# Attention scores of a hybrid decoder trunk: the keys' low parts meet the queries' high parts alone, for two heads at a time

## The chip, the cores and the metric

The kernel runs on one core of a Trainium2 chip. The metric is the time that one execution takes on the device, in microseconds. A core has five engines that work side by side, each with a queue of its own: TensorE (PE in the profile; its loads of the stationary operand are listed as PEld), VectorE (DVE), ScalarE (ACT), GpSimd (POOL) and SyncE (SP), which starts transfers. Matmuls write to PSUM, which the kernel uses as eight buffers of 128 partitions by 512 float32.

## What is computed

A trunk of two layers on a sequence of 512 tokens with 1024 features, in float32. Layer 0 mixes a gated linear recurrence and retention, layer 1 is sparse attention with three branches, and each layer ends with a SwiGLU block. The change is in the attention of layer 1 alone. Cut to that, for a block of queries (16 heads of 64 features in 4 groups of 4, keys and values shared by a group):

```python
s = einsum('bqgrd,bngd->bgrqn', qb, kc)            # compressed blocks
p_cmp = where(vis, softmax(where(vis, s, NEG)), 0)
...
s = einsum('bqgrd,bqgkld->bgrqkl', qb, kg)         # selected blocks
p_slc = softmax(where(ok, s, NEG))
...
s = einsum('bqgrd,bkgd->bgrqk', qb, kw)            # sliding window
p_win = softmax(where(band, s, NEG))
o = gate0 * o_cmp + gate1 * o_slc + gate2 * o_win
```

There are 512 / 64 = 8 blocks to select from, and up to 16 are selected, so all are; the window is 512 as well. The second and third branch are therefore plain causal attention, each with keys and values of its own.

## The kernel before

Matmuls run in a fast float32 form that keeps fewer bits, so an operand is split into a high part and a low part (the rest), and a product is made of three: high by high, high by low, low by high (`mm3`, L196 to L203). Weights are read from DRAM by SyncE's and GpSimd's queues and split by ScalarE and VectorE (`split`, L129).

**Keys and queries.** `layer1` (L937) makes the keys of the two causal branches. Each key head is written twice, in partitions 0 to 63 and again in 64 to 127 (`twice`, used at L1085), and the transposed tiles KH (high) and KL (low) are filled at L1099 to L1101. `stack` (L1113) writes the queries QS so that the two halves of the partitions hold different parts: an even head has its high part in partitions 0 to 63 and its low part in 64 to 127, an odd head the other way round (L1119 to L1122). One matmul over 128 partitions of QS against KH is thus high by high plus low by high; one against KL is high by low plus low by low.

**Units, heads, blocks.** `attention` (L1186) works through tiles i of 128 queries in the order 2, 3, 1, 0. A unit is a tile i, a group g and a set of branches: for i of 2 or 3 one branch (16 units in all), for i of 1 or 0 both branches side by side (8 units). A unit has four heads. With i + 1 blocks of 128 keys for each branch, a head's scores are 384 wide at i = 2, 512 at i = 3, 2 x 256 at i = 1 and 2 x 128 at i = 0. The steps of a head are:

- `head_s` (L1259): three matmuls into a PSUM buffer of the four behind `psA`: queries by KH (L1268), queries by KL (L1269), and the causal mask, added by an identity matmul on the last block of each branch (L1270);
- `head_m` (L1272): VectorE takes the negated row maximum (L1274);
- `head_e` (L1276): ScalarE's exponential with row sums, one for each branch (L1278);
- `scale` (L1285): GpSimd multiplies with the gate over the sum (L1288), a unit later.

The steps of a block of 128 keys, three units later (LAG at L1343), are `block_t` (L1290: four transposes into one of two PSUM buffers, L1293), `block_hi` (ScalarE's copy, L1297), `block_lo` (VectorE's subtraction, L1300, the last reader of that PSUM buffer) and `block_v` (L1303: two matmuls with the values, L1308 and L1309).

**Order.** The loop at L1346 to L1397 writes these steps slot by slot, a head (sl = 0 to 3) and a block in each slot:

```python
head_s(*hd)                      # slot sl of unit n
block_t(*bl)                     # a block of unit n - LAG
with prio(offset=12): head_m(*hd)
block_hi(*bl)
with prio(offset=-6): head_e(*hd)
with prio(offset=-12): block_lo(*bl)
```

Behind these, still in the slot, stand the scaling of the unit before, a `block_v`, steps of the compressed branch and of the finished outputs (`advance`), and, early in the stage, a piece of the queries' projection (`fill`, L201 to L203). This is not yet each engine's queue. When the program is built, a scheduler goes through its own forecast of the run and gives each engine the ready instruction that comes first in this order, shifted by the offsets of `prio`. A matmul that stands earlier but becomes ready late can thus be put between two that stand together here.

Two other places of the kernel matter for the change. `retention_core` (L613) multiplies 64-row halves at L633, for lower and upper partitions in turn, between full products at L650. The compression of keys has two small 64-row matmuls at L1055.

Of the kernel before, what the change touches and what calls it, by code (L numbers as in the profile page):

```python
# [19 lines left out]
AF = mybir.ActivationFunctionType  # L20
ALU = mybir.AluOpType
AX = mybir.AxisListType
PSUM = bass.MemoryType.PSUM

P = 128
# [10 lines left out]
DH = 64  # L36
# [27 lines left out]
class Trunk:  # L64
# [1121 lines left out]
    def attention(self, QS, stack, stacked, qlate, halves, KH, KL, VV, kc2, vc, gate, OH, OL, fill):  # L1186
# [3 lines left out]
        V, A, Q, T = nc.vector, nc.scalar, nc.gpsimd, nc.tensor  # L1190
# [52 lines left out]
        def late(t):  # L1243
            QS[t] = self.b8([P, H, P], F32R, name="qs")
            for c in range(2):
                stack(t, qlate[:, halves[1].index(t), 8 * c:8 * c + 8, :].rearrange("p h d -> p (h d)"), c)
                yield
# [11 lines left out]
        def head_s(u, r):  # L1259
            if r == 0:  # L1260
                u.p = self.probs().rearrange("p (r b x) -> p r b x", r=R, b=u.n)
                u.rs = self.sm.tile([P, R, u.n], F32, tag="rs", name="rs")
                u.kh, u.kl = (x[u.g // 2][:, u.bs[0]:u.bs[-1] + 1, u.g % 2, 0:u.nk] for x in (KH, KL))
            h = R * u.g + r
            ps = self.psA("ps_s")
            u.ps = ps[:, 0:u.n * u.nk].rearrange("p (b x) -> p b x", b=u.n)
            q = QS[u.i][:, h, :]
            T.matmul(u.ps, q, u.kh, start=True, stop=False)  # L1268
            T.matmul(u.ps, q, u.kl, start=False, stop=False)  # L1269
            T.matmul(u.ps[:, :, u.i * P:u.nk], self.identr, self.triNeg.unsqueeze(1).broadcast_to([P, u.n, P]), start=False, stop=True)  # L1270

        def head_m(u, r):  # L1272
            u.nm = self.sm.tile([P, 2], F32, tag="nm", name="nm")
            V.tensor_reduce(u.nm[:, 0:u.n], u.ps, axis=AX.X, op=ALU.max, negate=True)  # L1274

        def head_e(u, r):  # L1276
            for b in range(u.n):
                A.activation(u.p[:, r, b, 0:u.nk], u.ps[:, b, :], AF.Exp, bias=u.nm[:, b:b + 1], accum_out=u.rs[:, r, b:b + 1])  # L1278

        def norm(u):  # L1280
            gb = gate[:, u.i, :].rearrange("p (h b) -> p h b", b=3)[:, R * u.g:R * u.g + R, u.bs[0] + 1:u.bs[-1] + 2]
            V.reciprocal(u.rs, u.rs)
            Q.tensor_tensor(u.rs, u.rs, gb, op=ALU.mult)

        def scale(u, r):  # L1285
            for b in range(u.n):
                x = u.p[:, r, b, 0:u.nk]
                Q.tensor_tensor(x, x, u.rs[:, r, b:b + 1].broadcast_to([P, u.nk]), op=ALU.mult)  # L1288

        def block_t(u, b, j):  # L1290
            u.pt = self.psC("ps_tr")
            for r in range(R):
                T.transpose(u.pt[:, r * P:(r + 1) * P], u.p[:, r, b, j * P:(j + 1) * P], self.ident)  # L1293
            u.th, u.tl = (self.g2([P, S], F32R, name="pt" + n) for n in "hl")

        def block_hi(u, b, j):
            A.copy(u.th, u.pt)  # L1297

        def block_lo(u, b, j):
            V.tensor_tensor(u.tl, u.pt, u.th.bitcast(F32), op=ALU.subtract)  # L1300
            u.last = u.th, u.tl

        def block_v(u, b, j, th, tl):  # L1303
            br = u.bs[b]
            k = (u.i, u.g)
            if br == 0 and j == 0:
                out_ps[k] = self.psB("ps_o")
            T.matmul(out_ps[k], VV[br][:, j, u.g, :], th, start=(br == 0 and j == 0), stop=False)  # L1308
            T.matmul(out_ps[k], VV[br][:, j, u.g, :], tl, start=False, stop=False)  # L1309
            if br == 1 and j == u.i:  # L1310
                while u.i not in cmp_pt:
                    advance()
                ch, cl = cmp_pt[u.i]
                T.matmul(out_ps[k], vc[:, u.g, :], ch, start=False, stop=False)
                T.matmul(out_ps[k], vc[:, u.g, :], cl, start=False, stop=True)

        def finish(i, g):
            po = out_ps.pop((i, g))
            up = self.g2([P, S], name="up")
            A.copy(up[0:DH], po[DH:P])  # L1320
            yield
            o = self.g2([P, 2, P], name="o")
            p5, u5 = (x.rearrange("p (k z c) -> p k z c", k=2, z=2) for x in (po, up))
            for par in range(2):
                V.tensor_tensor(o[par * DH:(par + 1) * DH], p5[0:DH, :, par, :], u5[0:DH, :, par, :], op=ALU.add)
            yield
            c = slice(2 * (g % 2), 2 * (g % 2) + 2)
            oh, ol = (x[g // 2][:, c, i * P:(i + 1) * P] for x in (OH, OL))
            A.copy(oh, o)
            yield  # L1330
            Q.tensor_tensor(ol, o, oh.bitcast(F32), op=ALU.subtract)
            yield
# [5 lines left out]
        def advance():  # L1338
            if side and next(side[0], 0) == 0:
                side.pop(0)  # L1340
                advance()
# [4 lines left out]
        for n in range(len(units) + LAG):  # L1346
            us = units[n] if n < len(units) else None
            if n >= len(units):

                self.plan("w1o", n - len(units), 2048)  # L1350
                self.load()
                self.prefetch(2)
            un = units[n - 1] if 0 <= n - 1 < len(units) else None
            uv = units[n - LAG] if n >= LAG else None
            if us is not None and us.g == us.bs[0] == 0:
                at = tiles.index(us.i)
                if at + 1 < NT:
                    t = tiles[at + 1]
                    side += ([late(t)] if t in halves[1] else []) + [compressed(t)]
            nb = len(uv.blocks) if uv else 0  # L1360
            for sl in range(max(R, nb)):
                hd = us.heads[sl] if us and sl < R else None
                bl = uv.blocks[sl] if sl < nb else None
                while us and (us.i, us.g // 2) not in stacked:
                    if next(fill, 0) == 0:
                        advance()
                if hd:
                    head_s(*hd)
                if bl:
                    block_t(*bl)  # L1370
                if hd:
                    with prio(offset=12):
                        head_m(*hd)
                if bl:
                    block_hi(*bl)
                if hd:
                    with prio(offset=-6):
                        head_e(*hd)
                if bl:
                    with prio(offset=-12):  # L1380
                        block_lo(*bl)
                if un and sl < R:
                    if sl == 0:
                        with prio(offset=-6):
                            norm(un)
                    scale(un, sl)
                if len(pend) >= 2:
                    args = pend.pop(0)
                    block_v(*args)
                    u, b, j = args[:3]  # L1390
                    if u.bs[b] == 1 and j == u.i:
                        side.insert(0, finish(u.i, u.g))
                if bl:
                    pend.append(bl + uv.last)
                for _ in range(2 if len(side) > 2 else 1):
                    advance()
                next(fill, 0)  # L1397
# [139 lines left out]
```

## Time and profile before

| | |
|---|---|
| median of the runs | 1241.33 us (3 runs, 1240.74 to 1241.51) |
| the profiled execution, its own time | 1242.66 us |
| its span in the trace | 1240.9 us |
| TensorE busy | 1212.4 us, 98% of the span |
| VectorE, ScalarE, GpSimd busy | 70%, 61%, 22% |
| first and last start of a score matmul (L1268) | 674.3 and 831.4 us |

The span is what the trace covers, from the first to the last instruction; the execution's own time has a little more around it. A row of the trace gives a start and a duration. A matmul's duration holds the time until its result has left the array, so matmuls in a row overlap in these rows: what one occupies is the distance from its start (or end) to the next one's. Ends of matmuls are modelled by the profiler. The tile shapes 128*128 and 64*128 behind a matmul's name are the rows and columns of the array that it uses, so 64*128 is a product over 64 partitions.

### The profile page before, as it was taken

The numbers are of one execution on the slowest core, as the hardware profiler recorded it, in microseconds if no ns is written. First come the engines' busy times: TensorE is split into PE (matmuls) and PEld (weight loads), VectorE is DVE, ScalarE is ACT, GpSimd is POOL, SyncE is SP. The second block draws the span as 40 slices with busy tenths as digits, with TensorE's granted clock in tenths as the row PEclk, the third lists the DMA queues.
The fourth block names the chain that finished last, engine by engine and source line by source line (L and its number), as shares of the span: only waits on it lengthen the run. The fifth ranks groups of instructions, "written<-read, shape, count | busy, mean of one in ns | idle before, by whom it ended". The sixth has DMA issues, their size and how long they took to land.

```text
span 1240.9 us, 16873 instructions
## 1 busy us (share of the span) xinstructions
PE 1212.4 (98%) x6045; PEld 1017.4 (82%) x6045; DVE 865.1 (70%) x1333; ACT 755.1 (61%) x1531; POOL 272.6 (22%) x351
## 2 busy tenths in 40 slices
PE   9999999999999999999999999999999999999996
PEld 8788888888878888987888878877888888888986
DVE  6886638658765876775264889985965966695764
ACT  6541347666666765655454688995776756675553
POOL 0001420221111113200000567681111211113300
PEclk9999999999999999999999999999999999999999
DMA  9231143787988799952100000124588798889932
GB/s 343 68 102 68 35 170 102 174 186 193 219 213 175 170 241 246 244 195 77 68 35 1 1 1 1 35 96 169 133 181 195 171 244 205 175 165 252 251 91 68
DMA packets 48788, 178.64 MB, mean 144 GB/s; under 512 B 5408, under 2 KB 7728, under 8 KB 40384
## 3 DMA queue, kind: packets, MB, share of 16 engines
q0 software_dynamic: 20928, 68.25, 30.2%
q1 hardware_dynamic: 27632, 109.27, 24.8%
q8 instruction: 48, 0.79, 0.2%
q14 instruction: 36, 0.29, 0.1%
q10 hardware_dynamic: 144, 0.04, 0.0%
HBM read 164.95 MB, written 12.58 MB: 143 GB/s over the span
## 4 chain that ended last, share of the span: by engine, by line
PE 70%; DMA 11%; DVE 8%; ACT 6%; issue 3%; POOL 2%; DVEq 0%; POOLq 0%; ACTq 0%; SPq 0%
DMA wr<-wfg 6%; PE ps_t L201 5%; PE ps_t L203 5%; PE ps_t L202 5%; PE ps_X L201 5%; PE ps_X L202 5%; PE ps_X L203 5%; DMA wr<-wff 3%; PE ps_V L201 3%; PE ps_V L202 2%; DVE wlo L137 2%; PE ps_V L203 2%; ACT whi L136 2%; PE ps L201 2%; PE ps L203 2%
## 5 line engine op out<-in xcount | busy, mean ns | idle before, releaser
L137 DVE TENSOR_TENSOR wlo<-wr,whi 128x1024 fp32r<-128x1024 f32 (+1 forms) x296 | 342.1, 1159 | 219.5 <-ACT whi L136 215.9
L136 ACT CAST whi<-wr 128x512 fp32r<-128x512 f32 (+1 forms) x588 | 321.9, 596 | 270.8 <-PE ps_t L203 51.4
L161 POOL DMA_DIRECT2D wr<-wff x64 | 55.4, 866 | 286.3 <-DVE wlo L137 247.9
L201 PE MATMUL ps_t<-whi,hgh 128*128 128x512 f32 x288 | 114.8, 399 | 0.0
L202 PE MATMUL ps_t<-wlo,hgh 128*128 128x512 f32 x288 | 113.3, 394 | 0.0
L203 PE MATMUL ps_t<-whi,hgl 128*128 128x512 f32 x288 | 112.7, 391 | 0.0
L201 PE MATMUL ps_X<-whi,sg 128*128 128x512 f32 (+1 forms) x288 | 107.9, 375 | 1.4 <-DVE part L296 1.4
L203 PE MATMUL ps_X<-whi,sg 128*128 128x512 f32 (+1 forms) x288 | 107.0, 371 | 0.0
L202 PE MATMUL ps_X<-wlo,sg 128*128 128x512 f32 (+1 forms) x288 | 106.9, 371 | 0.0
L1288 POOL TENSOR_TENSOR prob<-prob,rs 128x384 f32<-128x384 f32 (+3 forms) x128 | 88.0, 721 | 1.9
L1278 ACT ACTIVATE prob<-ps_s,nm 128x384 f32<-128x384 f32 (+3 forms) x128 | 68.0, 539 | 15.7 <-DVE nm L1274 15.0
L201 PE MATMUL ps_V<-whi,sg 128*128 128x512 f32 (+1 forms) x192 | 72.0, 375 | 5.0 <-ACT part L288 5.0
L202 PE MATMUL ps_V<-wlo,sg 128*128 128x512 f32 (+1 forms) x192 | 71.3, 372 | 0.0
L203 PE MATMUL ps_V<-whi,sg 128*128 128x512 f32 (+1 forms) x192 | 71.2, 371 | 0.0
L203 PEld LDWEIGHTS ps_t<-whi,hgl 128*128 128x128 f32 x288 | 54.1, 188 | 11.5 <-issue 0.2
L201 PEld LDWEIGHTS ps_t<-whi,hgh 128*128 128x128 f32 x288 | 54.1, 188 | 11.5 <-ACT tok_v L524 0.6
L202 PEld LDWEIGHTS ps_t<-wlo,hgh 128*128 128x128 f32 x288 | 54.2, 188 | 10.6 <-issue 0.5
L201 PEld LDWEIGHTS ps_X<-whi,sg 128*128 128x128 f32 x288 | 54.1, 188 | 10.6 <-DVE part L296 2.4
L1274 DVE TENSOR_REDUCE nm<-ps_s 128x1 f32<-128x384 f32 (+3 forms) x96 | 56.8, 595 | 7.4 <-PE ps_s L1270 6.3
L203 PEld LDWEIGHTS ps_X<-whi,sg 128*128 128x128 f32 x288 | 54.1, 188 | 7.6
L202 PEld LDWEIGHTS ps_X<-wlo,sg 128*128 128x128 f32 x288 | 54.1, 188 | 7.4
L161 POOL DMA_DIRECT2D wr<-w2s x32 | 27.7, 864 | 141.5 <-DVE wlo L137 122.4
(359 smaller groups left out, 2971.1 us busy)
## 6 DMA issues: line engine op xcount, KB each, us to landing
wr<-wff POOLq DMA_DIRECT2D x64, 512.0 KB, 6.0
wr<-wff SPq DMA_DIRECT2D x24, 1024.0 KB, 4.9
wr<-w2s POOLq DMA_DIRECT2D x32, 512.0 KB, 5.7
wr<-w2s SPq DMA_DIRECT2D x12, 1024.0 KB, 4.8
wr<-wfg POOLq DMA_DIRECT2D x32, 384.0 KB, 7.3
wr<-w0t SPq DMA_DIRECT2D x10, 1024.0 KB, 6.1
wr<-w1t SPq DMA_DIRECT2D x10, 1024.0 KB, 4.8
wr<-wfg SPq DMA_DIRECT2D x12, 768.0 KB, 6.2
```

The costliest lines, as they stand in the source:

```text
L136: self.nc.scalar.copy(hi[:, c], x[:, c])
L137: self.nc.vector.tensor_tensor(lo, x, hi.bitcast(F32), op=ALU.subtract)
L161: self.nc.gpsimd.dma_start(x[:, c], more[:, c], accum_op=ALU.add)
L201: mm(ps, ah, bh, start=(first and k == 0), stop=False)
L202: mm(ps, ah, bl, start=False, stop=False)
L203: mm(ps, al, bh, start=False, stop=(last and k == n - 1))
L1274: V.tensor_reduce(u.nm[:, 0:u.n], u.ps, axis=AX.X, op=ALU.max, negate=True)
L1278: A.activation(u.p[:, r, b, 0:u.nk], u.ps[:, b, :], AF.Exp, bias=u.nm[:, b:b + 1], accum_out=u.rs[:, r, b:b + 1])
L1288: Q.tensor_tensor(x, x, u.rs[:, r, b:b + 1].broadcast_to([P, u.nk]), op=ALU.mult)
```

## The change

The product with KL now takes the queries' high part alone: 64 partitions, the lower half for an even head and the upper half for an odd one. The low by low product is thereby left out. The two heads of a pair are taken together. An even head's `head_s` issues only its product with KH. The odd head's issues its own product with KH, then the two 64-row products one behind the other (into the two heads' PSUM buffers), then the two masks. `head_m` and `head_e` of both heads follow in the odd slot, the two maxima ahead of `block_hi` and the two exponentials after it; the even slot has neither.

```diff
--- before.py
+++ after.py
@@ -1262,20 +1262,26 @@
                 u.rs = self.sm.tile([P, R, u.n], F32, tag="rs", name="rs")
                 u.kh, u.kl = (x[u.g // 2][:, u.bs[0]:u.bs[-1] + 1, u.g % 2, 0:u.nk] for x in (KH, KL))
             h = R * u.g + r
-            ps = self.psA("ps_s")
-            u.ps = ps[:, 0:u.n * u.nk].rearrange("p (b x) -> p b x", b=u.n)
-            q = QS[u.i][:, h, :]
-            T.matmul(u.ps, q, u.kh, start=True, stop=False)
-            T.matmul(u.ps, q, u.kl, start=False, stop=False)
-            T.matmul(u.ps[:, :, u.i * P:u.nk], self.identr, self.triNeg.unsqueeze(1).broadcast_to([P, u.n, P]), start=False, stop=True)
+            ps = self.psA("ps_s")[:, 0:u.n * u.nk].rearrange("p (b x) -> p b x", b=u.n)
+            T.matmul(ps, QS[u.i][:, h, :], u.kh, start=True, stop=False)
+            if r % 2 == 0:
+                u.even = ps
+                return
+
+            u.pair = u.even, ps
+            for z, x in enumerate(u.pair):
+                rows = slice(z * DH, (z + 1) * DH)
+                T.matmul(x, QS[u.i][rows, h - 1 + z, :], u.kl[rows], start=False, stop=False)
+            for x in u.pair:
+                T.matmul(x[:, :, u.i * P:u.nk], self.identr, self.triNeg.unsqueeze(1).broadcast_to([P, u.n, P]), start=False, stop=True)
 
         def head_m(u, r):
             u.nm = self.sm.tile([P, 2], F32, tag="nm", name="nm")
-            V.tensor_reduce(u.nm[:, 0:u.n], u.ps, axis=AX.X, op=ALU.max, negate=True)
+            V.tensor_reduce(u.nm[:, 0:u.n], u.pair[r % 2], axis=AX.X, op=ALU.max, negate=True)
 
         def head_e(u, r):
             for b in range(u.n):
-                A.activation(u.p[:, r, b, 0:u.nk], u.ps[:, b, :], AF.Exp, bias=u.nm[:, b:b + 1], accum_out=u.rs[:, r, b:b + 1])
+                A.activation(u.p[:, r, b, 0:u.nk], u.pair[r % 2][:, b, :], AF.Exp, bias=u.nm[:, b:b + 1], accum_out=u.rs[:, r, b:b + 1])
 
         def norm(u):
             gb = gate[:, u.i, :].rearrange("p (h b) -> p h b", b=3)[:, R * u.g:R * u.g + R, u.bs[0] + 1:u.bs[-1] + 2]
@@ -1368,14 +1374,18 @@
                     head_s(*hd)
                 if bl:
                     block_t(*bl)
-                if hd:
+                both = [(us, sl - 1), hd] if hd and sl % 2 else []
+                nms = []
+                for x in both:
                     with prio(offset=12):
-                        head_m(*hd)
+                        head_m(*x)
+                    nms.append(us.nm)
                 if bl:
                     block_hi(*bl)
-                if hd:
+                for x, us_nm in zip(both, nms):
+                    us.nm = us_nm
                     with prio(offset=-6):
-                        head_e(*hd)
+                        head_e(*x)
                 if bl:
                     with prio(offset=-12):
                         block_lo(*bl)
```

## Rows read from the trace of the kernel before

**Rows 1.** The page: engines' busy time, granted clock in 40 slices

```profile
PE 1212.4 (98%) x6045; PEld 1017.4 (82%) x6045; DVE 865.1 (70%) x1333; ACT 755.1 (61%) x1531; POOL 272.6 (22%) x351
...
PEclk9999999999999999999999999999999999999999
```

**Rows 2.** Windows: stretch, length, busy PE, PEld, DVE, ACT, POOL; clock, DMA share, GB/s

```profile
674.00:700.00 26.00, 25.74 (x143) 22.86 (x144) 19.50 (x40) 15.01 (x35) 7.96 (x11) 1.00 0.00 1
700.00:740.00 40.00, 36.14 (x232) 31.38 (x231) 34.80 (x76) 32.15 (x83) 26.92 (x38) 1.00 0.00 1
740.00:800.00 60.00, 59.14 (x361) 48.92 (x359) 56.52 (x106) 54.15 (x142) 42.79 (x56) 1.00 0.06 19
800.00:840.00 40.00, 38.20 (x236) 31.09 (x235) 35.08 (x74) 38.83 (x134) 32.89 (x70) 1.00 0.28 97
```

**Rows 3.** Waits of TensorE, 674 to 840 us: total us, times, longest

```profile
PE ps_tr L1236 <- POOL pcmp L1230: 1.7, 1, 1.7
PE ps_tr L1293 <- DVE ptl L1300: 1.7, 6, 0.6
...
PE ps_s L1268 <- DVE qs L1122: 1.1, 1, 1.1
...
PE ps_o L1309 <- DVE ptl L1300: 0.2, 1, 0.2
...
PE ps_s L1268 <- ACT prob L1278: 0.2, 1, 0.2
```

**Rows 4.** Groups by line and form, L1269: count, busy us, mean ns, idle before

```profile
L1269 PE MATMUL ps_s<-kl,qs 128*128 128x512 f32 x48 | 19.2, 399 | 0.0
...
L1269 PE MATMUL ps_s<-kl,qs 128*128 128x384 f32 x32 | 10.8, 338 | 0.0
...
L1269 PE MATMUL ps_s<-kl,qs 128*128 128x256 f32 x16 | 4.5, 281 | 0.0
```

**Rows 5.** Timeline of TensorE, three places: start us, duration us, instruction

```profile
609.80 0.39 PE L201 MATMUL ps_t<-whi,hgh 128*128 128x512 f32 x1
610.03 0.40 PE L202 MATMUL ps_t<-wlo,hgh 128*128 128x512 f32 x1
...
700.79 0.34 PE L1268 MATMUL ps_s<-kh,qs 128*128 128x384 f32 x1
700.97 0.34 PE L1269 MATMUL ps_s<-kl,qs 128*128 128x384 f32 x1
701.14 0.22 PE L1270 MATMUL ps_s<-triNeg,identr 128*128 128x128 f32 x1
...
822.63 0.28 PE L1269 MATMUL ps_s<-kl,qs 128*128 128x256 f32 x1
822.75 0.28 PE L1270 MATMUL ps_s<-triNeg,identr 128*128 128x256 f32 x1
```

**Rows 6.** Timeline of TensorE, retention in layer 0

```profile
109.67 0.60 PE L650 MATMUL ps_z<-tok_v,tok_k 128*128 128x128 f32 x4
110.20 1.16 PE L633 MATMUL ps_s<-tr_q,tr_k 64*128 64x128 f32 x16
111.30 0.71 PE L650 MATMUL ps_z<-tok_v,tok_k 128*128 128x128 f32 x4
```

**Rows 7.** Timeline of TensorE, the keys' compression in layer 1

```profile
609.10 0.43 PE L1055 MATMUL ps_c<-cw,hid 64*128 64x64 f32 x2
609.46 0.50 PE L203 MATMUL ps_t<-whi,hgl 128*128 128x512 f32 x1
```

**Rows 8.** Timeline of TensorE: first and last score product with others behind it

```profile
729.20 0.40 PE L1268 MATMUL ps_s<-kh,qs 128*128 128x512 f32 x1
730.17 0.63 PE L1293 MATMUL ps_tr<-ident,prob 128*128 128x128 f32 x4 [0.57 <-DVE ptl L1300]
...
827.82 0.28 PE L1268 MATMUL ps_s<-kh,qs 128*128 128x256 f32 x1
```

**Rows 9.** Groups of VectorE by line and form, 674 to 840 us: the widest maximum

```profile
L1274 DVE TENSOR_REDUCE nm<-ps_s 128x1 f32<-128x512 f32 x32 | 21.6, 683 | 2.6 <-PE ps_s L1270 2.1
```

## The prediction, made before the change was built

> **What bounds the kernel now.** I read the page's list of engines first: TensorE is busy for 98% of the span at a granted clock of 9 tenths or more in every slice, and no other engine is above 70% [rows 1]. Time added to TensorE's queue, or taken from it, should therefore come out in the span nearly one for one, unless the stage that the change touches differs. So I cut that stage, from 674 to 840 us, into four stretches [rows 2]. TensorE is busy 159.2 of 166 us there, VectorE 145.9 and ScalarE 140.1. This stage is less lopsided than the whole: in 740 to 800 VectorE runs at 56.5 of 60 us beside TensorE's 59.1, and in 800 to 840 ScalarE runs at 38.8 of 40 beside 38.2. Still, TensorE is the engine that the others keep pace with, and the granted clock is 1.00 throughout, that is 2.4 GHz. Last I asked what TensorE waits for: 1.7 us in its transposes for the low-part subtraction that frees their PSUM buffer, 0.2 us in a value product for such a subtraction, 0.2 us in a score product for an exponential, and most of the rest for the compressed branch's chain over GpSimd and for the first query tile [rows 3].
>
> **The change, part by part.** *Removed:* half of the time of the keys' low-part products, if two of them share a slot. There are 96, 48 of 512 columns, 32 of 384 and 16 of 256 [rows 4]. What one is worth is the distance from its start to the next one's, as a row's duration has the latency in it. That is 0.23 us for 512 columns (610.03 less 609.80), 0.18 for 384 and 0.12 for 256 [rows 5]. With 24, 16 and 8 pairs this is 24 x 0.23 + 16 x 0.18 + 8 x 0.12 = 9.4 us less.
>
> *Does a pair share a slot?* The kernel before has such pairs: the retention scores of layer 0 contract 64 rows, lower and upper half in turn, into two PSUM buffers. Four full-height products beside them take 0.60 us, of which about 0.27 is the first one's latency, so 0.11 each. Sixteen of the 64-row products go from the end of the full-height group before, 109.67 + 0.60 = 110.27, to 110.20 + 1.16 = 111.36, in 1.09 us, where one after the other would need 16 x 0.11 = 1.76 [rows 6]. So two share a slot: eight slots make 0.88. I take full sharing. The other bound is none, and the 9.4 us stay.
>
> *Added: the change of height.* In the same row 1.09 less 0.88 leaves 0.21 us, and it stands at the way in: the sixteen follow a full-height group without any row between. The way out shows the same: the next four full-height products end at 111.30 + 0.71 = 112.01, or 0.65 after the 64-row group, where 4 x 0.11 = 0.44 was due. Again 0.21 [rows 6]. That is not a property of short products: in layer 1 two 64-row products end at 609.10 + 0.43 = 609.53, and the full-height product of 512 columns behind them ends at 609.46 + 0.50 = 609.96, 0.43 later instead of 0.23 [rows 7]. Three places give 0.20 to 0.21 for each change between 64 and 128 rows. The Trainium skill, TensorEngine Tiling (Array Packing), section Tiling Modes, says that changing the tiling mode drains the engine; it gives no price, and the rows here price it. Before, the attention stage has no such change. After, each pair of heads has two: full-height score of the odd head, two 64-row products, full-height masks. That is 48 x 2 x 0.20 = 19.2 us more. The lower bound is nothing, as no row shows it for two 512-column products of this operand type; the upper one is the 0.21 of the rows, so 20.2.
>
> *Added: pairs that come apart.* The queue isn't the program's order: a matmul that was put earlier and becomes ready late goes between. Of the 96 heads, 12 have other matmuls between the high and the low product, the first at 729.20 (0.40 us long, then transposes at 730.17), the last at 827.82 [rows 8]. If the two low products come apart as often, that is one pair in eight, 6 of 48. Each then loses its sharing, 9.4 / 48 = 0.2 us, and pays two more changes of height, 0.4: 6 x 0.6 = 3.6 us. Bounds: none, and half of the pairs, 14.4.
>
> *Moved: maxima and exponentials.* The even head's maximum and exponential now stand one slot later, in a burst with the odd head's. VectorE does two maxima of 0.68 us back to back [rows 9], and the subtraction that frees the transposes' PSUM buffer is behind them; the transposes of the slot after next wait for it. ScalarE gets two exponentials behind one copy. No work is added on either, GpSimd's scaling works on the unit before, and no DMA is issued or moved past on SP or POOL. An even head also holds its score buffer, one of four, a slot longer; the exponential that frees one is waited for 0.2 us now [rows 3]. Bounds: nothing, and for each of 48 pairs a tenth of a maximum, some 3 us. I take nothing, as the same stage becomes longer on TensorE, which gives VectorE and ScalarE room.
>
> *Cover.* TensorE idles 166 less 159.2 = 6.8 us in the stage [rows 2]. Added TensorE time can replace the part that waits for VectorE and ScalarE, 1.7 + 0.2 + 0.2 = 2.1 us [rows 3]; the first query tile and the compressed chain are waited for all the same, as they come from work that isn't shortened. I take 2 us; the bounds are 0 and 6.8. When that cover is gone, each further tenth of a microsecond per pair is 4.8 us of span.
>
> *Sum.* -9.4 + 19.2 + 3.6 - 2 = +11.4 us. The profiled execution took 1242.66 us, of which its span is 1240.9; it stands 1.3 above the median of the runs, 1241.33. So 1242.66 + 11.4 = 1254.1 in its own terms, less 1.3 gives 1253 us.
>
> **The rivals.** *A: the change of height costs nothing here* (faster). The two low products are long, their weights are known early, and the load might slip in behind the running product. Then only the 9.4 us remain: 1241.3 less 9.4 is 1232. It decides at 9.4 / 96 = 0.10 us per change: below that the kernel is faster, above it slower. Against it stand the three places with 0.20 to 0.21, one of them beside 512-column products [rows 6, 7]; for it, that none has these operands on both sides. The Trainium skill, TensorE: Matmul & The Clock Gate, section Part 3: Packing small matmuls, gives a span of one product plus some 4 ns for each further tile and no term for entering or leaving; by it alone the result would be this rival's. Rows 6 agree with its sharing and contradict it at both ends of the group.
>
> *B: the pair doesn't share* (slower still). Either the long products stream one after the other in spite of their halves, or the queue pulls most pairs apart, so that the change doesn't do what it says. The 9.4 us stay: +11.4 + 9.4 = +20.8, or 1262 us. For it: one head in eight is split already [rows 8]. Against: the sixteen retention products [rows 6].
>
> *C: a draw.* The changes cost some 0.10 us each, or all of the 6.8 us of idle time and the room of the stretches where VectorE and ScalarE run level with TensorE take up most of the 9.8 us that are left without split pairs: 9.8 less 6.8 is +3, and a little less makes 1241 to 1244. Against it: in 674 to 700 TensorE is busy 25.7 of 26 us [rows 2], so the pairs there have no cover.
>
> **How the numbers follow.** The forecast has 0.68, with a range of its own from 1247 (no split pairs, full cover: -9.4 + 19.2 - 4) to 1260 (a quarter of the pairs split, no cover, some burst). A has 0.10, B 0.15, C 0.07. About 0.2%, 2.5 us, is what a measurement can tell from no change. Faster by more than that is A alone: 0.10; within it C: 0.07; slower is the rest: 0.83. The range from 1241 to 1264 leaves out A, half of C and the upper part of B, some 0.18 in all.
>
> **What would show it.** In the changed profile the 64-row products should stand two by two, starts 0.01 to 0.02 us apart, and the pair plus the first mask should take some 0.4 us longer from end to end than their columns. In the four stretches [rows 2] the granted clock stays at 1.00 and TensorE's busy share stays above 95% while the stage ends some 11 us later; everything behind it is moved by the same amount. If the first mask's end follows the pair's by about 0.06 us, as a mask does now (701.14 + 0.22 = 701.36 after 700.97 + 0.34 = 701.31, [rows 5]), the price is wrong and A holds. If the starts in a pair are a product's width apart, B holds. If TensorE's waits for maxima, exponentials or subtractions rise by more than 3 us in all, I mis-sized the burst.

## The result and the profile after

The changed kernel takes 1257.42 us (median of 4 runs, 1253.79 to 1260.03) against 1241.42 us before (4 runs). The ratio is 1.0121, with a 95% interval from 1.0106 to 1.0136: slower by 15 us (16 by the two medians; "over before" below goes by the ratio). The forecast was 1253 us with a range from 1241 to 1264.

The execution that was profiled took 1260.03 us, at the upper end of the runs. The page's engines and granted clock in 40 slices:

```profile
PE 1229.8 (98%) x6045; PEld 1014.1 (81%) x6045; DVE 864.9 (69%) x1333; ACT 755.1 (60%) x1531; POOL 272.6 (22%) x351
...
PEclk9999999999999999999999999999999999999998
```

The counts of instructions are those of [rows 1]; TensorE alone is busy longer, by 17.4 us, and the other engines are not. Windows of the changed kernel: the attention stage in the stretches of [rows 2], then two stretches elsewhere (length; busy time of PE, PEld, DVE, ACT, POOL; granted clock; DMA):

```profile
674.00:700.00 26.00, 23.64 (x117) 17.75 (x118) 16.41 (x36) 12.25 (x31) 7.46 (x11) 1.00 0.00 1
700.00:740.00 40.00, 39.41 (x225) 29.33 (x223) 33.14 (x71) 29.64 (x78) 24.93 (x36) 1.00 0.00 1
740.00:800.00 60.00, 58.35 (x320) 41.42 (x321) 50.76 (x94) 48.18 (x119) 39.04 (x47) 1.00 0.01 3
...
460.00:480.00 20.00, 18.15 (x96) 17.83 (x95) 9.43 (x12) 10.24 (x22) 7.85 (x9) 0.91 1.07 244
1160.00:1180.00 20.00, 19.44 (x107) 19.09 (x108) 14.16 (x21) 12.26 (x28) 7.73 (x9) 0.91 1.01 244
```

In 740 to 800 TensorE is as busy as before and does less: 320 matmuls instead of 361, with VectorE down from 56.5 to 50.8 us. This is how a slower TensorE looks here: its share doesn't move, the counts beside it do. The last two rows have nothing to do with the change: a mean of 0.91 over 20 us is a clock at 1.2 GHz, half speed, for 0.09 x 20 x 2 = 3.6 us in each, where the trace of before has 1.00. That is at most 1.8 us lost in each, so the profiled execution overstates the loss. The mean clocks of the four runs say the same: 0.994 and 0.995 in the runs of 1260.0 and 1259.1 us, 0.997 in those of 1253.8 and 1255.7.

To see the stage alone, I count each matmul from the end of the one before it to its own end, so that waits and changes count with the matmul that bears them. From the first score product to the last value product that makes 174.1 us before and 189.2 after, 15.1 more: the low products rise from 18.8 to 23.4 us, the masks from 7.7 to 17.8, the high products from 21.5 to 23.7, and all others together fall by 1.8.

Timeline of TensorE in the changed kernel: a pair that stands together, then one that came apart (L1266 is the high product, L1274 the low, L1276 the mask):

```profile
702.74 0.34 PE L1266 MATMUL ps_s<-kh,qs 128*128 128x384 f32 x1
703.01 0.45 PE L1274 MATMUL ps_s<-kl,qs 64*128 64x384 f32 x2
703.38 0.45 PE L1276 MATMUL ps_s<-triNeg,identr 128*128 128x128 f32 x2
...
715.32 0.44 PE L1274 MATMUL ps_s<-kl,qs 64*128 64x384 f32 x1
715.69 0.45 PE L1266 MATMUL ps_s<-kh,qs 128*128 128x384 f32 x1
716.07 0.43 PE L1274 MATMUL ps_s<-kl,qs 64*128 64x384 f32 x1
716.43 0.44 PE L1276 MATMUL ps_s<-triNeg,identr 128*128 128x128 f32 x2
```

The high product ends at 703.08 and the pair at 703.46: 0.38 us for two products of 384 columns, where one full-height product takes 0.18 [rows 5]. So the two share their slot, and the change of height costs 0.20. The two masks end 0.37 later instead of 0.06 + 0.11 = 0.17: another 0.20. Over the stage the trace has 36 pairs together, their starts 0.003 to 0.004 us apart, and 24 low products alone, that is 12 pairs apart. From the end of the matmul before, the first product of a 64-row group takes 0.42 us at 512 columns, 0.37 at 384 and 0.31 at 256 (medians), 0.19 above the 0.23, 0.18 and 0.12 of full-height products whatever the width; the first 128-column mask or transpose behind a group takes 0.26, where a mask took 0.06.

So far the profile tells a simple story: 120 changes of height at 0.195 us are 23.4, the 36 shared slots give back three quarters of 9.4, or 7.1, and the rest, 16, is the result. The experiments show that this sum is about right for TensorE's work, as low products and masks rise by 14.7 us together, and wrong as an account of the time.

### The profile page after: what moved, and what is told of

Read it like the earlier page. It is cut to its first block, busy times and chain, and to the rows that moved or that the text cites. A ratio compares the mean times of both kernels' runs of the same rounds, so it can differ in the third digit from the quotient of the medians.

```text
span 1258.3 us, 16875 instructions
## 1 busy us (share of the span) xinstructions
PE 1229.8 (98%) x6045; PEld 1014.1 (81%) x6045; DVE 864.9 (69%) x1333; ACT 755.1 (60%) x1531; POOL 272.6 (22%) x351
## 4 chain that ended last, share of the span: by engine, by line
PE 78%; DVE 7%; DMA 6%; ACT 5%; issue 3%; POOL 1%; DVEq 0%; POOLq 0%; ACTq 0%
PE ps_X L201 5%; PE ps_X L203 5%; PE ps_X L202 5%; PE ps_t L201 5%; PE ps_t L203 5%; PE ps_t L202 5%; PE ps_V L201 3%; PE ps_V L203 3%; PE ps_V L202 3%; PE ps_tr L1299 2%; DVE wlo L137 2%; PE ps_Z L201 2%; PE ps_Z L202 2%; PE ps_Z L203 2%; DMA wr<-w2s 2%
## 5 line engine op out<-in xcount | busy, mean ns | idle before, releaser
L1280 DVE TENSOR_REDUCE nm<-ps_s 128x1 f32<-128x384 f32 (+3 forms) x96 | 54.0, 594 | 13.7 <-PE ps_s L1276 13.1
L202 PEld LDWEIGHTS ps_t<-wlo,hgh 128*128 128x128 f32 x288 | 54.2, 188 | 10.6 <-issue 0.5
L1306 DVE TENSOR_TENSOR ptl<-ps_tr,pth 128x512 fp32r<-128x512 f32 x80 | 54.5, 684 | 11.3 <-ACT pth L1303 10.1
```

What stands on the lines that cost most here:

```text
L202: mm(ps, ah, bl, start=False, stop=False)
L1280: V.tensor_reduce(u.nm[:, 0:u.n], u.pair[r % 2], axis=AX.X, op=ALU.max, negate=True)
```

## Experiments

The first four had three theories. *Theory 1*: the time is that sum. *Theory 2*: the time comes from the order, that is the burst of two maxima and two exponentials and the score buffers that are held longer. *Theory 3*: half of each. All ratios are to the kernel before, run on the same chip.

| run | what it is | median us | ratio, 95% interval |
|---|---|---|---|
| changed kernel | | 1257.4 | 1.0121 [1.0106, 1.0136] |
| e1_full_height | pairs' order, low product with 128 rows | 1255.0 | 1.0114 [1.0095, 1.0134] |
| e2_half_alone | order of before, every low product 64 rows, alone | 1268.1 | 1.0217 [1.0202, 1.0233] |
| e3_kept_together | changed, all 48 pairs together | 1256.7 | 1.0121 [1.0105, 1.0138] |
| e5_four | four heads together | 1283.9 | 1.0347 [1.0325, 1.0369] |
| f1_burst_alone | matmuls of before, maxima and exponentials in pairs | 1244.1 | 1.0017 [1.0006, 1.0027] |
| f2_spread | e3, one maximum and exponential in a slot | 1256.4 | 1.0113 [1.0098, 1.0128] |
| f4_same_half | e3, both low products in one half | 1262.9 | 1.0162 [1.0145, 1.0179] |
| f3_odd_half | order of before, odd heads' low products 64 rows | 1252.0 | 1.0079 [1.0064, 1.0094] |
| g1_late_full | e1, both high products in the odd slot | 1250.5 | 1.0067 [1.0046, 1.0089] |
| g2_early_full | e1, both heads' matmuls in the even slot | 1247.5 | 1.0040 [1.0025, 1.0055] |
| g3_early_half | the same with 64 rows, 48 pairs together | 1254.9 | 1.0107 [1.0085, 1.0129] |
| h1_three_buffers | the kernel before with three score buffers | 1251.2 | 1.0067 [1.0050, 1.0084] |

### The order without the height, and the height without the order

e1_full_height, from the changed kernel:

```diff
-                rows = slice(z * DH, (z + 1) * DH)
-                T.matmul(x, QS[u.i][rows, h - 1 + z, :], u.kl[rows], start=False, stop=False)
+                T.matmul(x, QS[u.i][:, h - 1 + z, :], u.kl, start=False, stop=False)
```

> The pairs, the order of the maxima and exponentials and the scheduler stay as in the changed kernel, but the low product has all 128 rows again, as before. Theory 1 (the time goes to TensorE's change between 128 and 64 rows, 0.195 us each time): no change of height is left and none of the sharing, so TensorE has the work of the kernel before; 1241 to 1245 us. Theory 2 (the time goes to the burst: two maxima and two exponentials in one slot, and score buffers that are held longer): the burst is all there, so the time stays at 1250 to 1258 us. Theory 3 (half of each) lies at about 1249 us.

Measured: 14 us over before. Theory 1 falls. TensorE's own work in this kernel is that of before (low products 18.8 us, as there), yet by the medians almost the whole loss is there. In its trace the stage takes 182.8 us, 8.7 more: high products rise by 3.6, the first value products (L1308 before) by 3.8 and masks by 1.4 (a 128-column mask right behind another takes 0.11 us, behind a low product 0.06), with no work added to any of them. The two traced executions are only 10.6 us apart, as 1253.3 is the fastest of this kernel's four and 1242.66 lies above the median of before. These are TensorE's waits for the exponentials, copies and subtractions of the heads in e1 and then in the changed kernel (total us, times, longest):

```profile
PE ps_s L1266 <- ACT prob L1283: 2.4, 4, 1.6
PE ps_tr L1298 <- DVE ptl L1305: 2.2, 7, 0.8
PE ps_o L1313 <- ACT pth L1302: 2.2, 6, 0.7
...
PE ps_t L201 <- ACT prob L1283: 0.8, 1, 0.8
...
PE ps_o L1314 <- DVE ptl L1305: 0.5, 2, 0.3
```

```profile
PE ps_s L1266 <- ACT prob L1284: 1.7, 2, 1.4
...
PE ps_o L1314 <- ACT pth L1303: 1.0, 2, 0.7
PE ps_tr L1299 <- DVE ptl L1306: 1.0, 2, 0.8
...
PE ps_t L201 <- ACT prob L1284: 0.3, 1, 0.3
PE ps_o L1315 <- DVE ptl L1306: 0.2, 1, 0.2
```

That is 8.1 us in e1 and 4.2 in the changed kernel, where it was 2.1 before [rows 3].

e2_half_alone, from the kernel before:

```diff
-            T.matmul(u.ps, q, u.kl, start=False, stop=False)
+            rows = slice(h % 2 * DH, (h % 2 + 1) * DH)
+            T.matmul(u.ps, q[rows], u.kl[rows], start=False, stop=False)
```

> The kernel before in all its order, but each head's low product takes 64 rows where it stands, alone. Low by low is left out as in the changed kernel. Theory 1: 96 runs of one product, 192 changes of height at 0.195 us, no sharing: 37 us more, 1274 to 1280 us. Theory 2: the order is that of before, so 1241 us. If a change of height costs only where two low products stand together, also 1241 us.

Measured: 27 us over before, not 37. The price per change is as read. TensorE's timeline in this run, one head:

```profile
719.82 0.34 PE L1268 MATMUL ps_s<-kh,qs 128*128 128x384 f32 x1
720.09 0.44 PE L1270 MATMUL ps_s<-kl,qs 64*128 64x384 f32 x1
720.45 0.33 PE L1271 MATMUL ps_s<-triNeg,identr 128*128 128x128 f32 x1
```

720.16 to 720.53 is 0.37 for the low product alone (0.18 at full height), and 0.25 for a mask (0.05 to 0.06). Low products rise by 18.4 us and masks by 16.4. The difference to 27 is cover: with more work on TensorE, its transposes wait less (2.6 us), and so do the value products (1.5) and the compressed branch's transposes (2.8).

f3_odd_half does the same for odd heads alone (even ones keep all 128 rows):

```diff
-            T.matmul(u.ps, q, u.kl, start=False, stop=False)
+            rows = slice(DH, P) if r % 2 else slice(0, P)
+            T.matmul(u.ps, q[rows], u.kl[rows], start=False, stop=False)
```

> The kernel before in its order, with 64 rows for the odd heads' low products alone: 96 changes of height instead of the 192 of the run with every head, which was 27 us slower where the rows gave 37. In proportion: 13 to 14 us over the kernel before, 1254 to 1256 us. If the stage has a fixed reserve of some 10 us that is used up first: 96 x 0.195 = 18.7 less 10, so 1249 to 1251 us.

Measured: 9.8 us over before. The first 96 changes (18.7 us by the rows) cost 10, the next 96 cost 17. So the order of before holds a reserve of some 9 us, used up first; what comes after it goes into the time at nearly its full price (17 of 18.7 us).

### Keeping the pairs together, and taking their sharing away

e3_kept_together, from the changed kernel. At 715.32 above, the even head's low product goes ahead of the odd head's high product; 9 of the 12 pairs came apart so, the other three by transposes put between. The likely reason for the nine is that the scheduler, when it builds the queue, finds the low product ready and the high product still without a score buffer, as that product's operands are long there; no run took this alone apart.

```diff
-            T.matmul(ps, QS[u.i][:, h, :], u.kh, start=True, stop=False)
+            high = T.matmul(ps, QS[u.i][:, h, :], u.kh, start=True, stop=False)
...
-                T.matmul(x, QS[u.i][rows, h - 1 + z, :], u.kl[rows], start=False, stop=False)
+                with self.tc.high_priority(offset=60):
+                    self.after(T.matmul(x, QS[u.i][rows, h - 1 + z, :], u.kl[rows], start=False, stop=False), high)
```

> The changed kernel, but both low products are ordered behind the odd head's high product and given precedence, so that all 48 pairs stand together in TensorE's queue (36 do in the changed kernel, 12 came apart). Theory 1: 96 changes of height instead of 120 and 12 more shared slots, so 24 x 0.195 + 12 x 0.195 = 7 us less than the changed kernel: 1249 to 1252 us, which is 96 x 0.195 - 9.4 = 9 us over the kernel before. Theory 2: the burst is the same or stronger, as the even head's product waits longer: 1256 us or more.

Measured: 1256.7 us, no gain. The trace has all 48 pairs together, and low products and masks are back from 41.1 to 33.7 us; the profiled stage is only 2.5 us shorter (186.7). The rest went into waits: transposes rise by 2.0, first value products by 1.0, the compressed scores by 1.1.

f4_same_half puts both low products on the lower rows (the odd head's operand is then the query's low part):

```diff
-                rows = slice(z * DH, (z + 1) * DH)
+                rows = slice(0, DH)
```

> The pairs kept together, but both low products take the lower 64 rows, so they cannot share a slot; for the odd head these rows hold the query's low part, so the output is another. The starts in a pair should be a product's width apart (0.23, 0.18, 0.12 us) instead of 0.003 to 0.004. TensorE gets 9.4 us more than in the pairs kept together (1256.7 us). If the time follows TensorE's work: 1264 to 1267 us; if the waits of the pairs take it up: 1257 to 1261 us.

Measured: 1262.9 us, between the two. In the trace the two low products of a pair end a product's width apart (0.12, 0.18 and 0.23 us), and low products rise from 18.8 to 28.0 us, which is what sharing is worth; 5 to 6 of these 9.2 us come out in the time.

e5_four takes four heads together:

```diff
-            if r % 2 == 0:
-                u.even = ps
+            u.four = (u.four if r else ()) + (ps,)
+            if r < 3:
                 return
...
-            for z, x in enumerate(u.pair):
-                rows = slice(z * DH, (z + 1) * DH)
+            for z, x in enumerate(u.four):
+                rows = slice(z % 2 * DH, (z % 2 + 1) * DH)
...
-                both = [(us, sl - 1), hd] if hd and sl % 2 else []
+                both = us.heads if hd and sl == 3 else []
```

> Four heads at a time: the four high products, then the four low products of 64 rows in one run (two slots), then four masks, four maxima, four exponentials. Theory 1: 24 runs, 48 changes of height, 48 x 0.195 - 9.4 = 0 us in TensorE's work; what is added is waiting, since the four heads hold all four score buffers at once: 1242 to 1252 us, with more idle time of TensorE than in the changed kernel. Theory 2: the burst is twice as long as in the changed kernel, so over 1260 us.

Measured: 1283.9 us. The runs of four do what they should: low products fall to 14.6 us, the lowest of all kernels. The high products rise from 21.5 to 48.1 us. What a high product's row says of its waits in this run:

```profile
  ACT prob L1284: 40.1, 73
```

40.1 us in 73 waits (on TensorE and its weight loads together) until an exponential freed a score buffer; counted the same way it is 1.0 us in 4 waits in the kernel before, of which [rows 3] have TensorE's own 0.2. Not all of the 43 us that this kernel loses is its order: three stretches of its trace have a lower granted clock, where the attention stage before has 1.00 throughout [rows 2].

```profile
674.00:700.00 26.00, 22.64 (x104) 17.61 (x105) 12.77 (x30) 10.49 (x24) 3.39 (x5) 0.87 0.00 1
...
800.00:860.00 60.00, 51.18 (x271) 35.49 (x269) 43.06 (x84) 43.57 (x141) 33.37 (x58) 0.94 0.12 36
860.00:880.00 20.00, 16.84 (x90) 12.56 (x90) 13.78 (x29) 17.38 (x59) 12.60 (x31) 0.91 0.34 109
```

Counted as above, that is 17.6 us at half speed, so at most 9 us lost. When the clock first fell, at 684.4 us, TensorE stood in a wait of 2.26 us for an exponential.

### Which part of the order costs

Now *theory B* was the burst on VectorE and ScalarE, *theory C* the order on TensorE: the even head's scores are finished a slot late, together with the odd head's.

f1_burst_alone leaves every matmul as before:

```diff
+            u.pair = (u.pair[1] if r else None, u.ps)
...
-                if hd:
+                both = [(us, sl - 1), hd] if hd and sl % 2 else []
+                nms = []
+                for x in both:
                     with prio(offset=12):
-                        head_m(*hd)
+                        head_m(*x)
+                    nms.append(us.nm)
```

> All matmuls as in the kernel before, full height and each head's three in its own slot; alone the maxima and exponentials of a pair are taken together in the odd slot, as in the changed kernel. Theory B (the burst on VectorE and ScalarE with the even head's buffer held a slot longer is what costs in the full-height pairs): 1250 to 1256 us. Theory C (what costs there is the order on TensorE, the even head's scores that are finished a slot late, behind the odd head's): 1241 to 1244 us.

Measured: 2 us over before. So the place of the maxima and exponentials in the program is nearly free. But this kernel hardly makes the burst, as the scheduler still takes a maximum early when its scores are there. VectorE's timeline, in e1 and then in this run (x2 is two in a row, L1305 and L1301 are the subtraction):

```profile
714.65 1.02 DVE L1279 TENSOR_REDUCE nm<-ps_s 128x1 f32<-128x384 f32 x2
715.59 0.68 DVE L1305 TENSOR_TENSOR ptl<-ps_tr,pth 128x512 fp32r<-128x512 f32 x1
```

```profile
711.72 0.55 DVE L1275 TENSOR_REDUCE nm<-ps_s 128x1 f32<-128x384 f32 x1
712.18 0.68 DVE L1301 TENSOR_TENSOR ptl<-ps_tr,pth 128x512 fp32r<-128x512 f32 x1
712.95 0.56 DVE L1275 TENSOR_REDUCE nm<-ps_s 128x1 f32<-128x384 f32 x1
```

The two maxima of a pair follow each other directly in 37 of 48 pairs in e1 and in the changed kernel, in 13 here and in 6 before; and a score buffer is held no longer than before (3.48 us on average, 3.46 before, from the start of the high product to the end of the last exponential). So this run shows that theory B's reordering of the program costs little, and leaves the burst itself untested. f2_spread, from e3, takes the burst out of the other side:

```diff
-                both = [(us, sl - 1), hd] if hd and sl % 2 else []
+                if hd and sl % 2:
+                    waiting += [(us, sl - 1), hd]
+                both = [waiting.pop(0)] if waiting else []
```

> The changed kernel with all 48 pairs kept together, and one head's maximum and exponential in each slot: the even head's in the odd slot, the odd head's in the next even slot. Theory B: the burst is gone, the 96 changes of height with sharing stay (9 us of TensorE's work, part of it covered): 1245 to 1251 us. Theory C: the odd head comes later still and holds its score buffer longer: 1256 us or more, with longer waits of score products for exponentials.

Measured: 1256.4 us, as with the burst. In its trace 23 pairs of maxima still follow each other directly, 41 in e3. Half of the burst gone without a gain speaks against theory B; it does not settle it, as the odd head's buffer is held longer at the same time (4.60 us, 4.28 in e3). Theory C's second sign came weakly: high products stood 6.1 us for exponentials, counted as in e5 above, and 4.9 in e3.

What is left is when the scores come and how long their buffers are held. Two kernels move the matmuls of the full-height pairs (e1). g1_late_full draws the even head's high product into the odd slot:

```diff
-                if hd:
+                if hd and sl % 2:
+                    head_s(us, sl - 1)
                     head_s(*hd)
```

> Full-height pairs again, but with both high products in the odd slot, so that the even head's score buffer is no longer taken a slot before it is needed; its scores are ready as late as in the full-height pairs (1255 us). If the buffer that is held longer is the cost: 1241 to 1246 us. If the cost is that the even head's scores come late and both heads' at once: 1254 us or more.

g2_early_full draws the odd head's matmuls into the even slot, and each slot has its own head's maximum and exponential:

```diff
-                if hd:
-                    head_s(*hd)
+                if hd and sl % 2 == 0:
+                    head_s(us, sl)
+                    head_s(us, sl + 1)
...
-                both = [(us, sl - 1), hd] if hd and sl % 2 else []
+                both = [hd] if hd else []
```

> Full-height pairs with all matmuls of both heads in the even slot: the odd head's are drawn forward, no head's scores are late; the odd head's buffer is held up to a slot longer. Maximum and exponential of the even head in the even slot, of the odd head in the odd slot. If the even head's late scores are the cost: 1241 to 1245 us. If the buffer that is held longer is the cost: 1250 us or more.

Measured: 8 and 5 us over before, against 14 for e1. Neither theory holds alone. Not taking the even head's buffer a slot ahead gives back some 6 us (g1, where 39 pairs of maxima follow each other directly, 37 in e1). Drawing the odd head's matmuls forward gives back 9 (g2), but these pairs still cost 5; and as the even heads hold their buffers for less time in g2 too (3.75 us on average, 4.46 in e1), it does not price late scores alone. h1_three_buffers prices the buffers in the kernel before, which has no pairs:

```diff
+        taken = self.psA("taken")
+        V.memset(taken[:, 0:8], 0.0)
...
+        self.after(A.copy(self.s1([P, 8], "spare"), taken[:, 0:8]), self.last_exp)
```

> The kernel before with one of the four score buffers taken out of use, from the first score product to the last exponential (a small fill of it at the start and a small copy out of it at the end are added). If score buffers held longer are a large part of what the pairs cost (a pair's even head holds one for about a slot of every two, so half a buffer on average): 1246 to 1255 us. If buffers are not short: 1241 to 1244 us, and the pairs' cost is that both heads' scores come at once and ScalarE's copy for the value products stands behind their exponentials.

Measured: 8 us over before. Score buffers are short, and this is how it shows on a high product's row, the idle time before it that an exponential ended: first in this run, then in e1, then in the changed kernel (total us, times):

```profile
  ACT prob L1278: 10.0, 21
```

```profile
  ACT prob L1283: 6.9, 12
```

```profile
  ACT prob L1284: 4.6, 6
```

In g1 it is 4.1 us and in g2 1.9. The time for which a head holds its buffer, mean of the 96 heads, says the same: 3.46 us before, 3.48 in f1, 4.03 in g2, 4.08 in g1 and 4.35 in e1, in the order of what these kernels lose (2, 5, 8 and 14 us). Scores that come late keep their buffer longer too, so this does not part the two.

A second cost is on ScalarE. TensorE's waits in g1 and in e1, where the copy for the value products comes late:

```profile
PE ps_o L1313 <- ACT pth L1302: 3.7, 8, 0.7
```

```profile
PE ps_o L1313 <- ACT pth L1302: 2.2, 6, 0.7
```

[Rows 3] have no such wait. That the copies stand behind the exponentials of two heads is not what the traces show: 21 of the 80 copies in g1 and 18 in e1 come directly behind two heads' exponentials, and 21 did before. They start later after their transposes, 0.85 and 0.78 us on average against 0.66; why is open.

g3_early_half makes g2's edit, word for word, on e3_kept_together instead of e1_full_height, so it has 64 rows and all pairs together:

```diff
+                if hd and sl % 2 == 0:
+                    head_s(us, sl)
+                    head_s(us, sl + 1)
```

> The same order, pairs drawn forward, with the 64-row low products, all 48 pairs kept together: 96 changes of height, sharing, so TensorE has some 9 us more work than before. If late scores were what the changed kernel paid for besides: the height price less what the stage's reserve of some 9 to 10 us covers (96 changes alone cost 9.4 us without sharing, which is another 9.4 us): 1241 to 1247 us, under the changed kernel by 10 us. If the held buffer is the cost: 1254 us or more.

Measured: 1254.9 us, not the 1241 to 1247 that late scores as the only other cost would give. Over g2 it is 7 to 8 us, and TensorE's masks and low products rise by 7.9 (from 27.8 to 35.7): where the order costs less, the price of height comes out in full. No version here is faster than the kernel before.

## Why the prediction was right, and where its sum was not

**The sign, the price and the sharing** were right. The rows of retention and of the keys' compression gave 0.20 to 0.21 us for a change of height [rows 6, 7]; 0.19 to 0.20 was measured, for other operands and three widths. The two low products share a slot, starts 0.003 to 0.004 us apart. Rivals A and B fall by that, and C by the time. The Trainium skill, TensorEngine Tiling (Array Packing), Tiling Modes, says that changing the tiling mode drains the engine; the traces agree that a change costs time, 0.195 us each way. The span of a packed group that the Trainium skill gives in TensorE: Matmul & The Clock Gate, Part 3, has no such term; it agrees with the starts inside a pair, and leaves out what decides here: a pair of 512 columns wins 0.23 us and pays 0.39.

**Pairs that come apart**: the step took 6 from the rate in [rows 8]; it was 12, the quarter that the upper end of the range allowed for. In nine of them the even head's low product went ahead of the odd head's high product, an order that those rows, with heads one by one, cannot show.

**Moved: maxima and exponentials** is the step that failed. It took nothing for the order, and bounded it by 3 us. The order alone costs 14 (e1). Where the maxima and exponentials stand in the program, from which the bound was made, costs 2 (f1). The step should have followed the even head's scores. They wait for the odd head's buffer and high product, so that the even heads hold their buffers for 1.0 us longer in e1; the odd heads', on which it did not count, are held 0.8 longer. The bound rested on a wait of 0.2 us for an exponential [rows 3]. A wait that is short now says that four buffers are enough, and not that there is one to spare: taking one away costs 8 us (h1). The Trainium skill, TensorEngine Tiling (Array Packing), Restrictions and Gotchas, warns that row tiling raises the pressure on PSUM; here e1, which has no row tiling, shows that the pairs' order alone does so. The prediction's own sign for this step, a rise of TensorE's waits for maxima, exponentials and subtractions by more than 3 us, stayed silent in the changed kernel: 3.2 us without the copies, against 2.1. In e1, with the same order and less work on TensorE, it is 5.9.

**Cover** was mis-sized the other way: 2 us taken, 6.8 as the upper bound, some 9 measured in the order of before (f3: 18.7 by the rows, 9.8 in the time). The idle time that one view counts as waits was not all that gave way: in f3 transposes take 3.0 us less than before, those of the compressed branch 2.1 and the first value products 1.0. (The lower end of the range took 4 us as full cover, although this step's own bound is 6.8.)

So the mechanism of the height was right, and that 1253 came near 1257 is luck: errors against each other. In the sum's own terms the work added to TensorE was 16 us and not 13.4, as 12 pairs came apart; the order cost 14 and not nothing; and of these 30 only 15 are in the time, so 15 were covered and not 2. The last figure is a difference, and not a measurement of its own. A likely reading is that TensorE's new work fills time in which the pairs' order would have left it waiting: from e1 to the changed kernel these waits of TensorE fall from 8.1 to 4.2 us, high products by 1.4 and first value products by 3.1. It fits that e3, with 24 changes fewer, gains nothing, and that e1, with none, stands only 2 us lower by the medians, which is within the spread of the runs (in the two traces its stage is 6.4 us shorter, so the size of this difference is open).

**What is open**: how the 14 us of the order divide between buffers that are held longer, scores that come late, the burst that comes with them and ScalarE's late copies, and with that the 5 us that are left in g2.

## What to carry to other kernels

Look for the operation's own kind elsewhere in the trace: sixteen short products of another layer priced the change of height to within 0.02 us. A group of 64-row products between full-height ones pays about 0.39 us for going in and out, so it has to save more than that in one run. And where a stage has several engines near their limit, an added cost and a worse order don't add up; undo each alone before either is blamed, since a profile sum that fits the total, as 16 us did here, can still be the wrong account.

## What the runs showed of the hardware that was not expected

The price of a change of height doesn't depend on the width: 0.19 us on the way in at 256, 384 and 512 columns. And the granted clock can fall to its lower level, 1.2 GHz, for a few microseconds in a kernel that keeps TensorE 98% busy: the mean over 20 us was 0.91 twice in the changed kernel's profiled execution. Before each fall TensorE had waited for ScalarE (L288) and run again for 0.5 and 1.4 us. The changed kernel at both places; after the first fall a product of 384 columns takes 0.32 us from start to start, where 0.17 was usual:

```profile
471.97 0.45 PE L201 MATMUL ps_V<-whi,sg 128*128 128x384 f32 x1 [1.85 <-ACT part L288]
...
472.68 0.52 PE L201 MATMUL ps_V<-whi,sg 128*128 128x384 f32 x1
473.00 0.52 PE L202 MATMUL ps_V<-wlo,sg 128*128 128x384 f32 x1
...
1160.56 0.44 PE L201 MATMUL ps_V<-whi,sg 128*128 128x384 f32 x1 [2.77 <-ACT part L288]
```

In the kernel before the same two waits are shorter, and the clock stayed at 1.00:

```profile
471.75 0.44 PE L201 MATMUL ps_V<-whi,sg 128*128 128x384 f32 x1 [1.58 <-ACT part L288]
...
1143.33 0.44 PE L201 MATMUL ps_V<-whi,sg 128*128 128x384 f32 x1 [1.83 <-ACT part L288]
```

Whether that decides was not tried. The DMA engines were busy all through these windows (share 1.01 to 1.07), but that is not needed: in e5 the mean was 0.87 over 674 to 700 at a DMA share of 0.00.
